# Strassen's scheme for four more blocks of the first up projection and two more of the second, in a hybrid decoder layer

## The chip, the cores and the metric

The kernel runs on one core of a Trainium2 chip. The metric is the time of one execution on the device, in microseconds (us). The core has five engines with a queue each: PE (TensorE, the matmuls, with its weight loads shown apart as PEld), DVE (VectorE), ACT (ScalarE), POOL (GpSimd) and SP (SyncE, which here issues most of the DMAs).

## The reference

One decoder layer on 512 tokens of width 1024, all in float32. A vector c gives nine modulation rows (adaLN): a shift, a scale and a gate for each of three sublayers.

```python
mod = (cs @ w_ada[l] + b_ada[l]).reshape(bsz, N_MOD, D_MODEL)      # cs = silu(c)
h = modulate(x, sh1, sc1)
x = layer_norm(ALPHA * x + 0.5 * g1[:, None, :] * swiglu(h, ffn1_w1[l], ffn1_w3[l], ffn1_w2[l]), ...)
h = modulate(x, sh2, sc2)
m = hybrid_mixer(h, w_in[l], ...)         # SSD heads and S5 heads, one input and one output projection
x = layer_norm(ALPHA * x + g2[:, None, :] * m, ...)
h = modulate(x, sh3, sc3)
x = layer_norm(ALPHA * x + 0.5 * g3[:, None, :] * swiglu(h, ffn2_w1[l], ffn2_w3[l], ffn2_w2[l]), ...)

def swiglu(u, w1, w3, w2):
    return (jax.nn.silu(u @ w1) * (u @ w3)) @ w2                    # 1024 -> 2816 -> 1024
```

## The kernel before, in words

**Products.** A float32 product is made of three matmuls: each operand is split into a high part (a cast on ACT, in `split`, L96) and the rest (a subtraction on DVE, `tt`, L81), and `mm3` (L100) issues hi·hi (L103), hi·lo (L104) and lo·hi (L105) into one PSUM bank. Weights come in by DMA (`raw`), are split into `whi` and `wlo`, and go to PE as the stationary operand or the moving one.

**Stages, in order.** The first modulation and an early start of the up projection (to about 55 us); the first up projection, `up` (to 269.70); the first down projection, `down` (to 395.85), with the layer norm and the transposed, split tokens `hT` of the next sublayer (`to_h`); the mixer, which begins with the z projection from the weight tiles `zw`; the second up projection (its Strassen stage from 672.25 to 835.56); the second down projection.

**Up.** The 2816 hidden columns are 22 blocks of 128. For a block, `up` (L397) runs 8 steps along k, three matmuls of 512 columns each, for w1 and for w3 (48 in all), and `glue` multiplies silu of the one by the other into a half of a tile `g`. After each block it runs `per` steps from a list of jobs, generators that issue small pieces of other work. In the first up projection that job is the S5 setup (`s5_setup`, 71 steps, 4 a block); from block 11 on, `late` puts 3 steps a block of the list `ada` in its place. `ada` holds the loading of the residual and the other modulation rows: two pairs (shift and scale, `ada_pair`) and two gates (`ada_gate`), 70 steps. Each row is summed by `ada_acc` (L267): 8 loads of 512 KB into two tiles `ra`, each followed by a DVE instruction into `acc`. A gate is then split (`gs`), spread over the partitions by four matmuls with `onesr` (L318, L319) and added to its bias in the tile `gate`.

**Strassen.** `up_fast` (L477) does two blocks at a time, w1 or w3 (a unit): 7 products of quarter size in place of 8, each 4 steps along k by three matmuls of 256 columns, 84 in all. DVE makes the sums of weights (`wsum`, `raw`), and combines the products in the tile `cp`. The sums of tokens are made once (`h_sums`, tiles `hs`). Before, this is done for blocks 6 to 21 of the second up projection, 16 units.

**Down.** `down` (L629) makes two halves of 512 output columns, with four token tiles in four banks each, and runs `per` job steps per block (1 before). In the last 6 blocks of the second half the matmuls are held back and go token tile by token tile, so that each tile can be drained (`make_drain`: the gate product `dr`, the sum `res`, statistics `st` and `mv`, the normalisation) while PE works on the next.

**Order.** Each engine takes its own queue in order. The order in the queues is set by a scheduler of tiles from the program's order, priorities and when tiles come free; loads can be moved far ahead.

## Time and profile before

| | |
|---|---|
| median of 3 runs | 965.3 us (965.27 to 965.67) |
| profiled execution | 965.66 us |
| its span | 963.9 us |
| PE busy | 940.7 us (98%) |
| DVE busy | 759.0 us (79%) |
| ACT busy | 449.1 us (47%) |
| POOL busy | 34.0 us (4%) |
| granted clock of TensorE, mean | 0.995 |

The span runs from the first to the last instruction that the profiler records. An engine's busy time is the part of it in which the engine has an instruction under way; a matmul's row is longer than the distance to the next one's start, since matmuls are pipelined. In the rows below a number in square brackets is how long the engine stood idle ahead of an instruction, with what released it. The granted clock is a share of full speed (2.4 GHz). The page gives shares over the whole span, and single places are read from the timeline.

### The profile page before, as it was taken

Reading aid. Unit: us, or ns where it says so; the run is one execution under the profiler, and the core shown is the slowest. Engines: PE = TensorE matmul, PEld = TensorE weight load, DVE = VectorE, ACT = ScalarE, POOL = GpSimd, SP = SyncE. Lnnn points to the kernel's source line nnn. Section 1 sums busy time; section 2 is a strip of 40 time slices with the busy share of each in tenths; the row PEclk is TensorE's granted clock in tenths of the full one; section 3 lists DMA queues with packets and bytes.
Section 4 is the critical chain, followed back from the end, with each engine's and each line's share of the span. In section 5 each row is a group of like instructions: output and inputs, shape, how many; then the busy total and the mean of one; then the engine's idle time right before and its main releaser. Section 6 shows DMA issues by size and latency. Waiting matters only on the chain.

```text
span 963.9 us, 14718 instructions
## 1 busy us (share of the span) xinstructions
PE 940.7 (98%) x5409; PEld 797.0 (83%) x5409; DVE 759.0 (79%) x1522; ACT 449.1 (47%) x882; POOL 34.0 (4%) x73
## 2 busy tenths in 40 slices
PE   8999999999999999999999999999999999999996
PEld 5778888887777878778877777988999999988885
DVE  6579999963686897858995889885788888796946
ACT  3343452635453335545637945432455554634420
POOL 0000000000000000100000110100000000000003
PEclk9999999999999999999999999999999999999998
DMA  9967585453765765362432034521233232543302
GB/s 343 378 182 267 191 278 168 159 175 126 260 199 189 258 220 160 104 218 88 143 121 66 1 100 141 192 92 66 88 108 112 91 130 88 176 152 109 109 1 87
DMA packets 75577, 147.92 MB, mean 153 GB/s; under 512 B 11632, under 2 KB 28656, under 8 KB 74992
## 3 DMA queue, kind: packets, MB, share of 16 engines
q1 hardware_dynamic: 75216, 146.94, 46.1%
q8 instruction: 42, 0.69, 0.3%
q14 instruction: 31, 0.25, 0.1%
q10 hardware_dynamic: 288, 0.04, 0.0%
HBM read 137.52 MB, written 9.44 MB: 152 GB/s over the span
## 4 chain that ended last, share of the span: by engine, by line
PE 84%; DVE 6%; ACT 3%; issue 2%; DMA 2%; POOL 1%; SPq 0%; DVEq 0%; POOLq 0%; ACTq 0%
PE ps L103 27%; PE ps L104 27%; PE ps L105 27%; DMA ew<-in_up_dram 1%; DVE cv L90 1%; PE ps L980 1%; DVE wlo L81 1%; ACT whi L96 1%; DMA b_ada<-in_badaT_dram 1%; DVE s5X L81 0%; POOL rsx L170 0%; DMA raw<-in_w_in_dram 0%; PE ps L253 0%; PE ps L295 0%; DVE s5t L81 0%
## 5 line engine op out<-in xcount | busy, mean ns | idle before, releaser
L96 ACT CAST whi<-raw 128x1024 fp32r<-128x1024 f32 (+1 forms) x155 | 155.0, 1007 | 212.0 <-PE ps L104 98.4
L81 DVE TENSOR_TENSOR wlo<-raw,whi 128x1024 fp32r<-128x1024 f32 (+1 forms) x155 | 179.3, 1168 | 44.6 <-ACT whi L96 44.1
L103 PE MATMUL ps<-hT,whi 128*128 128x512 f32 x448 | 177.0, 396 | 2.4 <-ACT hT L1498 2.4
L104 PE MATMUL ps<-hT,whi 128*128 128x512 f32 x448 | 174.7, 390 | 0.1
L105 PE MATMUL ps<-hT,wlo 128*128 128x512 f32 x448 | 174.5, 390 | 0.0
L103 PE MATMUL ps<-whi,ghl 128*128 128x512 f32 x320 | 125.2, 391 | 0.0
L104 PE MATMUL ps<-wlo,ghl 128*128 128x512 f32 x320 | 124.5, 389 | 0.0
L105 PE MATMUL ps<-whi,ghl 128*128 128x512 f32 x320 | 124.3, 389 | 0.0
L103 PEld LDWEIGHTS ps<-hT,whi 128*128 128x128 f32 x448 | 83.9, 188 | 23.9 <-issue 3.2
L105 PEld LDWEIGHTS ps<-hT,wlo 128*128 128x128 f32 x448 | 84.1, 188 | 17.8
L104 PEld LDWEIGHTS ps<-hT,whi 128*128 128x128 f32 x448 | 84.2, 188 | 17.1 <-DVE hT L81 0.5
L103 PE MATMUL ps<-hx,whi 128*128 128x256 f32 (+1 forms) x320 | 97.5, 305 | 0.7 <-DVE cp L90 0.6
L104 PE MATMUL ps<-hx,whi 128*128 128x256 f32 (+1 forms) x320 | 97.4, 304 | 0.0
L105 PE MATMUL ps<-hx,wlo 128*128 128x256 f32 (+1 forms) x320 | 97.3, 304 | 0.0
L90 DVE SCALAR_TENSOR_TENSOR acc<-ra,cs,acc 128x1024 f32<-128x1024 f32 (+2 forms) x62 | 71.0, 1145 | 19.3 <-DMA ra<-in_w_ada_dram 18.6
L96 ACT CAST ghl<-g 128x512 fp32r<-128x512 f32 x88 | 53.2, 619 | 50.1 <-PE ps L105 38.8
L103 PEld LDWEIGHTS ps<-whi,ghl 128*128 128x128 f32 x320 | 60.1, 188 | 14.8 <-issue 2.5
L105 PEld LDWEIGHTS ps<-whi,ghl 128*128 128x128 f32 x320 | 60.1, 188 | 12.7
L104 PEld LDWEIGHTS ps<-wlo,ghl 128*128 128x128 f32 x320 | 60.1, 188 | 12.1
L81 DVE TENSOR_TENSOR ghl<-g,ghl 128x512 fp32r<-128x512 f32 x88 | 58.2, 687 | 12.7 <-ACT ghl L96 12.7
L103 PEld LDWEIGHTS ps<-hx,whi 128*128 128x128 f32 x320 | 61.1, 191 | 3.9 <-issue 0.8
L105 PEld LDWEIGHTS ps<-hx,wlo 128*128 128x128 f32 x320 | 61.2, 191 | 2.5
(471 smaller groups left out, 1690.9 us busy)
## 6 DMA issues: line engine op xcount, KB each, us to landing
ra<-in_w_ada_dram SPq DMA_DIRECT2D x56, 512.0 KB, 4.5
raw<-in_up_dram SPq DMA_DIRECT2D x49, 512.0 KB, 4.3
raw<-in_ffn_w_dram SPq DMA_DIRECT2D x44, 512.0 KB, 4.2
raw<-in_up_dram SPq DMA_DIRECT2D x64, 256.0 KB, 3.8
ra<-in_ada_dram SPq DMA_DIRECT2D x16, 512.0 KB, 7.8
...
```

The costliest lines, as they stand in the source:

```text
L81: self.nc.vector.tensor_tensor(out=out, in0=a, in1=b, op=op)
L90: self.nc.vector.scalar_tensor_tensor(out=out, in0=a, scalar=s, in1=b, op0=op0, op1=op1, **k)
L96: keep(self.nc.scalar.copy(out=hi, in_=src))
L103: mm(o, lh, rh, start=first, stop=False, **k)
L104: mm(o, lh, rl, start=False, stop=False, **k)
L105: self.last_mm = mm(o, ll, rh, start=False, stop=last, **k)
L980: nc.tensor.matmul(pv[32 * r:32 * r + 32, j, :], M[:, n, r, 32 * j:32 * j + 32], rhs[:, r, :], start=(n == 0), stop=(n == 2))
```

## The change

Blocks 18 to 21 of the first up projection are done by `up_fast` (`FAST1 = 18`), 4 units; in the second up projection the Strassen stage begins at block 4 rather than 6 (`FAST = 4`), 18 units. The S5 setup goes at 6 steps a block, its scratch is released before the sums of tokens take their space, and the `ada` list starts at block 13 (`late=(ada, 3, 13)`). Beside blocks 16 and 17 run the sums of tokens and the first loads and sums of weights (`lead`). During the 4 units one `ada` step follows each unit, and `down` takes 7 `ada` steps in 5 blocks. `cp` moves from the pool of temporaries to pools of its own, `g` tiles can come from a list of spares, and `identr` is cast on ACT in the mixer rather than on DVE at the start. The branches with `add` are not taken; the sums and splits of weights of a unit stay as they were, and their functions are left out below.

```diff
--- before.py
+++ after.py
@@ -381,10 +382,13 @@
             yield
+    def g_tile(self, gp):
+        return self.spare.pop(0) if self.spare else gp.tile([P, 2, S], F32, tag="g", bufs=NF // 2, name=self.nm("g"))
     def glue(self, gp, g, f, pa, pb):
...
         if f % 2 == 0:
-            self.gt = gp.tile([P, 2, S], F32, tag="g", bufs=NF // 2, name=self.nm("g"))
+            self.gt = self.g_tile(gp)
         s = self.tmp.tile([P, 512], F32, tag="t2", name=self.nm("sl"))
@@ -540,9 +550,9 @@
                 self.tt(gt[:, 0, 256:512], gt[:, 0, 256:512], bank[:, 0:256], MUL)
-        load(0)
-        yield
-        load(1)
+        load(0, 0), load(0, 1)
+        yield
+        load(1, 0), load(1, 1)
         yield
@@ -552,14 +562,16 @@
             if j == 0:
-                gt = gts.pop() if gts else gp.tile([P, 2, S], F32, tag="g", bufs=NF // 2, name=self.nm("g"))
+                gt = self.g_tile(gp)
                 g.extend((gt[:, 0, :], gt[:, 1, :]))
-            cp = self.tmp.tile([P, 4, 256], F32, tag="t4", name=self.nm("cp"))
+            cp = sp.tile([P, 3, 256], F32, tag="cp", bufs=2, name=self.nm("cp"))
             p1, u2, p5 = [cp[:, n] for n in range(3)]
...
             prep_c(u)
+            if add:
+                load(u + 2, 0)
             C = self.bank()
@@ -567,14 +579,14 @@
                 prep_a(u + 1)
-            else:
+            elif not add:
                 last()
-            prep_d(u)
-            if u + 2 < len(units):
-                load(u + 2)
+            if not add:
+                prep_d(u)
+                load(u + 2, 0), load(u + 2, 1)
             prod(u, A, "t2", new[1], False)
             nc.scalar.copy(out=u2, in_=A[:, 0:256])
-            self.step(jobs, 1)
+            self.step(jobs, per)
             B = self.bank()
@@ -643,7 +662,8 @@
                                  f == 0, f == nk - 1)
-                    self.step(jobs, per)
+                    slot += 1
+                    self.step(jobs, slot * per // 5 - (slot - 1) * per // 5)
             for t in range(NT):
@@ -1085,6 +1105,8 @@
         nc.scalar.copy(out=self.mask4, in_=bc(self.mask, (1, 4)))
+        self.identr = dp.tile([P, P], F32R, name="identr")
+        nc.scalar.copy(out=self.identr, in_=self.ident)
         for g in range(2):
@@ -1099,8 +1121,6 @@
                                 pattern=[[-1, P]], channel_multiplier=1)
-        self.identr = self.cp.tile([P, P], F32R, name="identr")
-        nc.vector.tensor_copy(self.identr, self.ident)
         self.hsel = self.cp.tile([NC * NH, NH], F32, name="hsel")
@@ -1446,10 +1466,11 @@
         L.early = len(L.wq)
-        L.want_up(ins['up1'], EARLY)
         TAIL = 4
         HALVES = 2
-        FAST = 6
+        FAST1 = 18
+        FAST = 4
+        L.want_up(ins['up1'], EARLY, nf=FAST1)
         def g_alloc():
@@ -1462,10 +1483,14 @@
         g1, g2, g3, m2, m3 = [], [], [], [], []
-        L.want_down(NF, ins['ffn1_w2'][0])
-        L.wlimit = len(L.wq)
-        L.want_mixer()
-        L.want_up(ins['up2'], (), HALVES, g_alloc, FAST)
+        wsum = [L.gates.tile([P, 1024], F32, tag="gate", bufs=2, name="wsum1")]
+        def down1():
+            L.want_down(NF, ins['ffn1_w2'][0])
+            L.wlimit = len(L.wq)
+            L.want_mixer()
+            L.want_up(ins['up2'], (), HALVES, g_alloc, FAST)
+            L.wahead(L.wi + 2)
         hctx, gctx, pctx, fctx, xctx = [ExitStack() for _ in range(5)]
@@ -1538,11 +1563,26 @@
             L.glue(gp, g, f, pss[f, 0], pss[f, 1])
+        L.spare = [L.g_tile(gp) for _ in range(NF // 2 - (len(g) + 1) // 2)]
         jobs = [L.s5_setup(pre)]
         ada = [xres(), L.ada_gate(2, 0.5, g1), L.ada_pair(3, m2), L.ada_pair(6, m3), L.ada_gate(5, 1.0, g2)]
-        L.up(hT, gp, g, f0, jobs, 4, late=(ada, 3, 11), done=pss[f0, 0])
+        L.up(hT, gp, g, f0, jobs, 6, late=(ada, 3, 13), done=pss[f0, 0], nf=FAST1 - 2)
         L.step(jobs, 1000)
         pctx.close()
+        sctx = ExitStack()
+        sp = sctx.enter_context(tile_pool("f1"))
+        hs = [sp.tile([P, 2, 4, 2, P], F32R, tag="hs", bufs=3, name=f"hs1{k}") for k in range(3)]
+        quarter = lambda k, t: hT[:, 2 * t:2 * t + 2, 4 * k:4 * k + 4]
+        z = L.tmp.tile([P, 1024], F32, tag="t4", name="hsum").rearrange("p (a q) -> p a q", a=2)
+        jobs = [L.h_sums(quarter, hs, L.spare[-2:] + [z])]
+        fast = L.up_fast(quarter, hs, wsum[0], sp, gp, g, ins['up1'], FAST1, down1, ada, 1)
+        lead = [(next(fast) for _ in range(4))]
+        L.up(hT, gp, g, FAST1 - 2, jobs, 4, late=(lead, 4, FAST1 - 1), nf=FAST1)
+        L.step(jobs, 1000)
+        L.step(lead, 4)
+        next(fast)
+        ada.insert(0, fast)
+        sctx.close()
         def ln_cols(lg, lb, m):
@@ -1575,7 +1615,7 @@
             L.to_h(hT2, t, res[t], *GB)
-        L.down(NF, getl_of(g, gl), L.make_drain(res, lambda: g1[0], ln1), 6, ada, 1)
+        L.down(NF, getl_of(g, gl), L.make_drain(res, lambda: g1[0], ln1), 6, ada, 7)
         L.step(ada, 1000)
@@ -1602,11 +1642,17 @@
             L.wahead(L.wi + 2)
-        gts = []
-        jobs = [L.h_sums(hx, hs, fp, gts), L.ada_gate(8, 0.5, g3)]
-        fast = L.up_fast(hx, hs, fp, gts, g, ins['up2'], FAST, down2, jobs)
+        wsum2 = L.gates.tile([P, 1024], F32, tag="gate", bufs=2, name="wsum2")
+        quarter = lambda k, t: hx[k][:, 2 * t:2 * t + 2]
+        def sums():
+            own = [L.g_tile(fp) for _ in range(3)]
+            yield from L.h_sums(quarter, hs, own)
+            L.spare = own
+        jobs = [sums(), L.ada_gate(8, 0.5, g3)]
+        fast = L.up_fast(quarter, hs, wsum2, sp, fp, g, ins['up2'], FAST, down2, jobs, 1)
         lead = [(next(fast) for _ in range(4))]
-        L.up(hT3[0], fp, g, 0, jobs, 4, halves=HALVES, late=(lead, 4, FAST - 1), nf=FAST)
+        L.up(hT3[0], fp, g, 0, jobs, 5, halves=HALVES, late=(lead, 4, FAST - 1), nf=FAST)
         L.step(lead, 4)
```

Line numbers of the change are up to 1 higher than before in the places quoted here. Three places show how the queues move.

DVE at the end of the first down projection, before: the last split of `g` (`ghl`), the four splits of the z weights, and the first drain (`dr`).

```order
L81 TENSOR_TENSOR ghl_3849<-g_2880,ghl_3849 128x512
L81 TENSOR_TENSOR zw_4024<-raw_3784,zw_4024 128x1024
L81 TENSOR_TENSOR zw_4027<-raw_3828,zw_4027 128x1024
L81 TENSOR_TENSOR zw_4030<-raw_3836,zw_4030 128x1024
L81 TENSOR_TENSOR zw_4035<-raw_3844,zw_4035 128x1024
L81 TENSOR_TENSOR dr_3870<-ps_3481,gate_1847 128x512
L81 TENSOR_TENSOR wdtr<-wdt,wdtr 128x8x8
```

DVE after the last drain, in the change: the tokens' last `hT` for the first tiles, the normalisation of the last token tile (`res_122`), the split of the attention gate's sum (`gs`, from `acc_3970`), its two additions into `gate_3968`, and the first splits of the z weights.

```order
L82 TENSOR_TENSOR hT_3172<-tf_4225,hT_3172 128x4x128
L88 TENSOR_SCALAR res_122<-res_122,mv_4252,rs_4254 128x1024
L88 TENSOR_SCALAR tf_4225<-ps_4237,G_4168,B_4169 128x128
L86 TENSOR_SCALAR gate_6628<-gate_6628 128x1024
L82 TENSOR_TENSOR hT_3172<-tf_4225,hT_3172 128x4x128
L82 TENSOR_TENSOR gs_4263<-acc_3970,gs_4262 128x1024
L91 SCALAR_TENSOR_TENSOR gate_3968<-ps_4266,gate_3968 128x512
L91 SCALAR_TENSOR_TENSOR gate_3968<-ps_4270,gate_3968 128x512
L82 TENSOR_TENSOR zw_4279<-raw_4023,zw_4279 128x1024
L82 TENSOR_TENSOR zw_4282<-raw_4068,zw_4282 128x1024
```

The z splits stand behind all four drains and behind the end of the attention gate; before, they stood ahead of the first drain.

PE at the same place, before: the last down matmul, eight transposes, the first z matmuls.

```order
L105 MATMUL ps_3484<-whi_3824,ghl_3849 128x512
L339 MATMUL ps_3986<-ident,res_121 128x128 x4
L339 MATMUL ps_3997<-ident,res_121 128x128 x4
L103 MATMUL ps_4059<-zw_4024,hT_2995 128x512
L104 MATMUL ps_4059<-zw_4024,hT_2995 128x512
```

The same in the change.

```order
L106 MATMUL ps_3705<-whi_4064,ghl_4089 128x512
L340 MATMUL ps_4226<-ident,res_120 128x128 x4
L340 MATMUL ps_4237<-ident,res_120 128x128 x4
L319 MATMUL ps_4266<-gs_4262,onesr 128x512
L319 MATMUL ps_4270<-gs_4262,onesr 128x512
L320 MATMUL ps_4266<-gs_4263,onesr 128x512
L320 MATMUL ps_4270<-gs_4263,onesr 128x512
L104 MATMUL ps_4314<-zw_4279,hT_3172 128x512
L105 MATMUL ps_4314<-zw_4279,hT_3172 128x512
```

Four matmuls of the gate (`gs` by `onesr`) stand between the transposes and the first z matmul.

DVE in the first unit of the new Strassen stage, in the change (`acc` is the modulation row, `cp` combines the products, `ps_2688` is the bank that the unit's last product needs, `wlo`, `wsum` and `raw` are weights).

```order
L91 SCALAR_TENSOR_TENSOR acc_3259<-ra_3305,cs,acc_3259 128x1024
L82 TENSOR_TENSOR wlo_2729<-raw_2620,whi_2728 128x512
L91 SCALAR_TENSOR_TENSOR acc_3259<-ra_3308,cs,acc_3259 128x1024
L82 TENSOR_TENSOR cp_2687<-cp_2687,ps_2754 128x256
L91 SCALAR_TENSOR_TENSOR cp_2687<-cp_2687,ps_2707 128x256
L91 SCALAR_TENSOR_TENSOR acc_3259<-ra_3326,cs,acc_3259 128x1024
L82 TENSOR_TENSOR wlo_2783<-raw_2641,whi_2782 128x1024
L91 SCALAR_TENSOR_TENSOR cp_2687<-cp_2687,ps_2688 128x256
L82 TENSOR_TENSOR wlo_2816<-wsum_113,whi_2815 128x1024
L82 TENSOR_TENSOR raw_2641<-raw_2641,wsum_113 128x512
```

Three accumulations of `acc_3259`, each with a load of its own, stand among the unit's splits and combinations.

## Rows read from the trace of the kernel before

**Rows 1.** Page: busy us (share of the span) and instructions of each engine.
```profile
PE 940.7 (98%) x5409; PEld 797.0 (83%) x5409; DVE 759.0 (79%) x1522; ACT 449.1 (47%) x882; POOL 34.0 (4%) x73
```

**Rows 2.** Stretches: busy us (count) of PE, PEld, DVE, ACT, POOL; clock, DMA, GB/s.
```profile
90.00:100.00 10.00, 10.00 (x46) 8.29 (x45) 10.00 (x54) 3.78 (x12) 0.00 (x0) 1.00 0.79 274
...
700.00:750.00 50.00, 50.00 (x419) 50.00 (x418) 42.14 (x62) 27.05 (x44) 0.00 (x0) 1.00 0.32 106
270.00:396.00 126.00, 126.00 (x562) 101.54 (x561) 102.24 (x132) 56.84 (x82) 1.59 (x4) 1.00 0.63 198
```

**Rows 3.** Timeline of PE, first up projection: start, us, instruction.
```profile
59.83 0.39 PE L105 MATMUL ps<-hT,wlo 128*128 128x512 f32 x1
...
72.30 0.39 PE L103 MATMUL ps<-hT,whi 128*128 128x512 f32 x1
```

**Rows 4.** Timeline of PE, Strassen stage of the second up projection.
```profile
699.73 0.28 PE L103 MATMUL ps<-hx,whi 128*128 128x256 f32 x1
...
711.25 0.28 PE L103 MATMUL ps<-hs,whi 128*128 128x256 f32 x1
```

**Rows 5.** Timeline of PE, end of that stage (in brackets: idle before, releaser).
```profile
833.52 0.28 PE L105 MATMUL ps<-hs,wlo 128*128 128x256 f32 x1
834.41 0.36 PE L103 MATMUL ps<-hx,whi 128*128 128x256 f32 x1 [0.61 <-DVE cp L90]
...
835.56 0.40 PE L103 MATMUL ps<-whi,ghl 128*128 128x512 f32 x1
...
837.64 0.39 PE L103 MATMUL ps<-whi,ghl 128*128 128x512 f32 x1
```

**Rows 6.** Timeline of PE, end of the first up projection.
```profile
269.47 0.39 PE L105 MATMUL ps<-hT,wlo 128*128 128x512 f32 x1
269.70 0.39 PE L103 MATMUL ps<-whi,ghl 128*128 128x512 f32 x1
```

**Rows 7.** Waits of DVE (us, times, longest us); instructions on tile `ra`, 276 to 300.
```profile
DVE acc L90 <- DMA ra<-in_w_ada_dram: 18.6, 18, 3.4
...
L90 DVE SCALAR_TENSOR_TENSOR acc<-ra,cs,acc x7: 1280/1285/1286, 277.1 to 295.2; 128x1024 f32<-128x1024 f32 x7
...
DMA to landing us min/median/max: 3.6/4.4/5.0
```

**Rows 8.** Groups of DVE, 45 to 290: busy us, mean ns, idle before, releasers.
```profile
L81 DVE TENSOR_TENSOR wlo<-raw,whi 128x1024 fp32r<-128x1024 f32 x43 | 52.3, 1221 | 12.1 <-ACT whi L96 11.9
```

**Rows 9.** Timeline of DVE, end of the first down projection.
```profile
378.65 4.63 DVE L81 TENSOR_TENSOR zw<-raw,zw 128x1024 fp32r<-128x1024 f32 x4 [1.11 <-ACT zw L96]
...
395.93 0.68 DVE L672 BATCH_NORM_STATS2 st<-res 128x6 f32<-128x512 f32 x1
396.53 0.39 DVE L87 TENSOR_SCALAR tf<-ps,G,B 128x128 f32<-128x128 f32 x1
396.84 0.20 DVE L675 BATCH_NORM_AGGREGATE mv<-st 128x2 f32<-128x12 f32 x1
...
398.04 0.81 DVE L87 TENSOR_SCALAR res<-res,mv,rs 128x1024 f32<-128x1024 f32 x1 [0.72 <-POOL rs L171]
...
399.36 0.69 DVE L81 TENSOR_TENSOR dr<-ps,gate 128x512 f32<-128x512 f32 x1
```

**Rows 10.** Timeline of PE, from the first down projection to z.
```profile
395.85 1.03 PE L339 MATMUL ps<-ident,res 128*128 128x128 f32 x8
397.63 0.50 PE L103 MATMUL ps<-zw,hT 128*128 128x512 f32 x1 [0.74 <-ACT hT L96]
...
399.50 0.50 PE L105 MATMUL ps<-zw,hT 128*128 128x512 f32 x1 [1.14 <-DVE hT L81]
```

**Rows 11.** PE after a gap in the mixer (timeline), and stretches with their clock.
```profile
493.85 0.65 PE L980 MATMUL ps<-s5X,s5M 128*32 128x128 f32 x8 [2.08 <-DVE s5X L81]
...
397.00:400.00 3.00, 1.23 (x4) 0.75 (x5) 2.28 (x6) 3.00 (x7) 0.79 (x2) 1.00 0.00 0
494.00:497.00 3.00, 3.00 (x60) 3.00 (x59) 3.00 (x5) 1.30 (x2) 0.00 (x0) 0.50 0.42 153
```

More of the change, by code (lines that the diff above doesn't have):

```diff
@@ L436, in up, with h_sums @@
                 pss.append(ps)
-    def h_sums(self, hq, new, gp, gts):
+    def h_sums(self, v, new, gts):
         nc = self.nc
-        v = lambda k, t: hq[k][:, 2 * t:2 * t + 2]
         hi, lo = lambda a: a[:, :, :, 0, :], lambda a: a[:, :, :, 1, :]
-        for _ in range(3):
-            gts.append(gp.tile([P, 2, S], F32, tag="g", bufs=NF // 2, name=self.nm("g")))
         x, y, z = [t.rearrange("p a (b q) -> p (a b) q", q=P).rearrange("p (t k) q -> p t k q", t=2)
@@ L475, in h_sums, with up_fast, load @@
         self.s4 = lambda: split(y, v(0, 1))
-    def up_fast(self, hq, new, gp, gts, g, w, f0, last, jobs):
+    def up_fast(self, v, new, c, sp, gp, g, w, f0, last, jobs, per, add=False):
         nc = self.nc
         units = [(f, j) for f in range(f0, NF, 2) for j in range(2)]
-        v = lambda k, t: hq[k][:, 2 * t:2 * t + 2]
         raws, ops, hold = {}, {}, {}
-        def load(u):
+        def load(u, kh):
+            if u >= len(units):
+                return
             f, j = units[u]
-            ts = []
-            for kh in range(2):
-                t = self.raw.tile([P, 1024], F32, tag="raw", name=self.nm("raw"))
-                for m in range(2):
-                    nc.sync.dma_start(out=t[:, 512 * m:512 * m + 512].rearrange("p (k n) -> p k n", k=4),
-                                      in_=w[f + m][:, j, 4 * kh:4 * kh + 4])
-                ts.append(t)
-            raws[u] = ts
+            t = self.raw.tile([P, 1024], F32, tag="raw", name=self.nm("raw"))
+            for m in range(2):
+                x = t[:, 512 * m:512 * m + 512].rearrange("p (k n) -> p k n", k=4)
+                nc.sync.dma_start(out=x, in_=w[f + m][:, j, 4 * kh:4 * kh + 4])
+            if add and kh == 0:
+                nc.gpsimd.dma_start(out=x, in_=w[f][:, j, 0:4], accum_op=ADD)
+            raws.setdefault(u, []).append(t)
         def split(u, raw, names):
@@ L506, in up_fast @@
         lo_, hi_ = slice(0, 512), slice(512, 1024)
-        c = self.gates.tile([P, 1024], F32, tag="gate", bufs=2, name="wsum")
         def prep_a(u):
             a, b = raws[u]
-            self.tt(c[:, lo_], a[:, hi_], b[:, hi_], ADD)
-            self.tt(a[:, hi_], a[:, hi_], a[:, lo_], ADD)
+            if not add:
+                self.tt(c[:, lo_], a[:, hi_], b[:, hi_], ADD)
+                self.tt(a[:, hi_], a[:, hi_], a[:, lo_], ADD)
             split(u, a, ("b11", "t1"))
-            self.tt(c[:, hi_], a[:, hi_], b[:, hi_], ADD)
+            if not add:
+                self.tt(c[:, hi_], a[:, hi_], b[:, hi_], ADD)
         def prep_b(u):
-            split(u, raws[u][1], ("b21", "b22"))
+            a, b = raws[u]
+            if add:
+                self.tt(c[:, hi_], a[:, hi_], b[:, hi_], ADD)
+                self.tt(c[:, lo_], c[:, hi_], a[:, lo_], SUB)
+            split(u, b, ("b21", "b22"))
+            if add:
+                nc.gpsimd.dma_start(out=b[:, lo_], in_=c[:, hi_], accum_op=ADD)
         def prep_c(u):
             split(u, c, ("t3", "t2"))
-            b = raws[u][1]
-            self.tt(b[:, lo_], b[:, lo_], c[:, hi_], ADD)
+            if not add:
+                b = raws[u][1]
+                self.tt(b[:, lo_], b[:, lo_], c[:, hi_], ADD)
         def prep_d(u):
@@ L562, in up_fast @@
             prep_c(u)
+            if add:
+                load(u + 2, 0)
             C = self.bank()
@@ L569, in up_fast @@
                 prep_a(u + 1)
[L570 removed]
+            elif not add:
                 last()
[L572 to L574 removed]
+            if not add:
+                prep_d(u)
+                load(u + 2, 0), load(u + 2, 1)
             prod(u, A, "t2", new[1], False)
             nc.scalar.copy(out=u2, in_=A[:, 0:256])
[L577 removed]
+            self.step(jobs, per)
             B = self.bank()
@@ L584, in up_fast @@
                 self.tt(gt[:, 0, 0:256], gt[:, 0, 0:256], p1, MUL)
+            if add:
+                prep_d(u)
+                load(u + 2, 1)
             prod(u, C, "b22", v(0, 1), False)
@@ L588, in up_fast @@
                 prep_b(u + 1)
+            elif add:
+                last()
             prod(u, A, "t3", new[2], False)
@@ L627, in want_down, with down @@
                           (lambda sl=sl: gate()[:, sl]) if gate and hf == 1 else None)
-    def down(self, nk, getl, drain, tail, jobs=None, per=1):
+    def down(self, nk, getl, drain, tail, jobs=None, per=5):
+        slot = 0
         for hf in range(2):
```

1 line of the change is left out of this document (added).

## The prediction

> **What bounds the kernel now.** I began with the busy shares of the page. PE (TensorE) is busy for 940.7 of 963.9 us and VectorE (DVE) for 759.0 [rows 1]. So the time is PE's work plus the 23 us in which PE stands still, and a change is worth what it takes off PE's queue less what it makes PE wait. The stretches say which engine would be next. In the first up projection (90 to 100) PE and DVE are both full; in the Strassen stage (700 to 750) DVE runs 42.14 of 50 us; in the first down projection (270 to 396) PE is never idle and DVE has 102.24 of 126 [rows 2]. PE's waits are therefore looked for where a stage ends, and DVE's where a load is late.
>
> The profiled execution took 965.66 us, 1.76 outside its span, and 0.36 above the median of 965.3. The sum is made against 965.66, and 0.36 comes off at the end. Of this kernel no more than 0.2%, 1.9 us, can be told from no change.
>
> **Matmuls removed: -4.8 us.** One unit (two blocks, one of w1 and w3) costs 48 x 512 columns directly and 84 x 256 columns by Strassen. In a full stretch the 512-column matmuls start at 59.83 and, 55 later, at 72.30: 0.2267 us each [rows 3]. The 256-column ones start at 699.73 and, 96 later, at 711.25: 0.120 each [rows 4]. A unit goes from 48 x 0.2267 = 10.88 to 84 x 0.120 = 10.08 and saves 0.80; four new units in the first up projection and two in the second save 4.8.
>
> The Trainium skill ("TensorE: Matmul & The Clock Gate", section "Wait — 56ns, not 53.3ns?") gives start-to-start as the columns over 2.4 GHz and about 2.5 ns more, which is 215.7 ns for 512 and, worked out the same way, an estimate of 109.2 for 256. By it a unit would save 48 x 0.2157 - 84 x 0.1092 = 1.18 us and the six 7.1. The trace has both slower, and the 256-column ones by more; the trace decides.
>
> **Closing a second Strassen stage: +0.9 us (0.5 to 1.5).** The last product of the last unit waits for the subtraction that frees its bank: the matmul expected at 833.64 starts at 834.41, 0.77 lost. From there to 835.56 the rows show starts at 0.12 with 0.07 on top, and from 835.56 to 837.64 nine 512-column matmuls, 2.04 us worth in 2.08 [rows 5]. The kernel before goes from up to down in block form without such a gap: 269.47, then 269.70 [rows 6]. So the price is new.
>
> **Inside that stage: +1.3 us (0 to 4).** DVE's sums and splits for Strassen are joined by accumulations for adaLN (`acc<-ra`), which wait on their loads with everything behind them waiting too. In the second up projection few such loads fall among the units. Here, by the order shown above, `acc_3259<-ra_3326` stands right ahead of the subtraction into `cp_2687` that frees the bank for the next unit's closing product. PE reaches that product 2.88 us (24 x 0.120) after the subtraction's input is done. The accumulations waited 18.6 us in all for their loads, the worst 3.4 [rows 7]. A wait of 3.4 and two instructions of 1.2 in the way exceed 2.88 by about 3, once; usually it fits. I take 1.3, between none and the 4 us of two bad waits, nearer to none, since 18.6 us over 18 waits is one each.
>
> **S5 setup at 6 steps a block: 0 (0 to 3).** The same instructions run, earlier; the adaLN work starts 2 blocks later and gives its place up (8 accumulations less, some 10 us, between blocks 3 and 13). What hides it: PE in the first up projection shows no wait, and DVE's weight splits in that stage themselves wait for casts (11.9 us `<-ACT whi`) [rows 8], so they run ahead of PE. If that cover goes, PE pays DVE's excess directly. The larger step of 5 jobs in the second up projection and the moved cast of `identr` go with it, at 0: the sums there run beside 512-column matmuls with DVE under its limit.
>
> **From the down projection to the mixer: +6.7, and +3 (0 to 7) on top.** Before, `ada` is done well inside the down projection. Before DVE's first drain stand the four splits of the z weights: 378.65, 4.63 us [rows 9]; so when the last down matmul ends (E = 395.85) PE needs just the normalised tokens. It starts z at 397.63, waits once more, and has the third z matmul at 399.50 [rows 10]; counted back two matmuls of 0.23, z runs as if it had started at 399.04, E + 3.2.
>
> After, 70 adaLN steps are to be done: 9 beside blocks, 4 in the Strassen units, and 38 x 7/5 = 53 in the down projection. That is 66. The last four, the end of the attention gate, come behind the down projection: PE's queue has the four gate matmuls between the last down matmul and z, and DVE's queue has all four drains and this gate ahead of the z splits. From E on DVE must do, in order, with durations from [rows 9] less 0.085, by which rows that follow each other overlap (395.93, 0.68 long, and the next at 396.53): drain 0.60, add 0.60, `tf` 0.32, statistics 0.60 and 0.13, `hT` 0.60, the scaling 0.73 after a wait for POOL of up to 1.00 (0.72 there), `tf` 0.32, gate scale 0.60, `hT` 0.60, the gate split 1.14, a start of PE and its result 0.5, two additions 1.20, and the z split 1.14: 10.1 us. Only z's second matmul needs that split, so z starts at E + 9.9, and 9.9 - 3.2 = **+6.7**. That holds if DVE is not behind at E. The last two accumulations stand between the drains, and each waits for a load. 17 more of them lie between the first half's drains and the second half's first. Before, seven in a row came from 277.1 to 295.2, 3.0 us apart, with loads of 4.4 us into two buffers [rows 7]: 51 us for the 17. The half lasts 126.15/2 = 63.1 and its first drain comes 12.7 before its end (three tiles of 18 matmuls and the transposes): 50.4. So they come out about even, and any longer wait pushes the drains. I add 3, less than one load of 4.4, between 0 and one and a half loads.
>
> **The clock: +1.5 (0 to 2).** After 2.08 us of standing still PE's granted clock was 0.50 (1.2 GHz of 2.4) from 494 to 497, 3 us in which half was lost, 1.5. After the shorter gaps at 397 to 400 it stayed at 1.00 [rows 11]. The new gap is longer than either, so I take the first.
>
> **Sum:** -4.8 + 0.9 + 1.3 + 0 + 6.7 + 3 + 1.5 = +8.6; 965.66 + 8.6 - 0.36 = **973.9 us**. With the low ends (0.5, 0, 0, 6.7 less 1 for pieces that may overlap, 0, 0) it is 966.7; with the high ends (1.5, 4, 0, 6.7, 7, 2) it is 981.7. Likeliest case's own range: 967 to 982.
>
> **Rival 1, faster: a 256-column matmul costs half of a 512-column one.** Place: the six units. If 0.120 is not the engine's pace but that of the Strassen stage's operands, and new units run at 0.2267/2 = 0.1133, a unit takes 9.52 and saves 1.36; six save 8.2. With the low ends of closing (0.5) and transition (5.7) this gives 965.3 - 8.2 + 6.2 = 963.3. It decides below a pace of about 0.116. The page named above has the halves at 109.2, which speaks for it; against it stand 96 steps on end at an even 0.120 [rows 4]. Chance 0.10.
>
> **Rival 2, no difference.** DVE is up to date at E, the clock does not fall, the Strassen stage closes at 0.5 and has no wait inside: 965.3 - 4.8 + 0.5 + 5.7 = 966.7. For it: two accumulations less before the drains than I fear, and 4.63 us of z splits no longer ahead of them. Chance 0.10.
>
> **Rival 3, much slower: DVE saturates in the first up projection.** At 90 to 100 it already runs 10.00 of 10 [rows 2], and six steps of S5 a block add half as much again. If the weight splits fall behind, PE waits in up to 13 blocks; at 1 us a block that is 973.9 + 13 = 986.9. Against it: [rows 8], and fewer accumulations. It decides if the splits' waits for ACT vanish. Chance 0.08. That the change skips work is not a rival: its queue holds 6 x 84 matmuls for 6 x 48.
>
> **Chances.** Likeliest 0.72, rival 1 0.10, rival 2 0.10, rival 3 0.08. Below 963.4: rival 1's better half and a little from better ends, 0.11. Within 963.4 to 967.2: 0.10. Slower: 0.79. The range goes from 963.0, just past rival 1, to 982; rival 3 is left out.
>
> **What would show it.** The units of the first up projection take 10.08 us each; between PE's last down matmul and its first z matmul lie gate matmuls and 8 to 15 us; DVE's z splits start after all drains; granted clock 0.50 follows. A gap under 5 us there, or PE waits before block 13, would prove the sum wrong.

## The result and the profile after

The changed kernel takes 987.8 us (median of three, 987.5 to 990.0) against 965.3: ratio 1.0233, 95% interval 1.0219 to 1.0246. The forecast was 973.9 with a range to 982; the side was right, the size was not. The profiled execution's span is 985.8 us, 21.9 longer than before.

The page of the kernel after, busy time by engine and the granted clock in 40 slices (tenths of full speed):

```profile
PE 943.8 (96%) x5625; PEld 807.2 (82%) x5625; DVE 801.3 (81%) x1590; ACT 471.3 (48%) x920; POOL 34.3 (3%) x73
...
PEclk9999899999999999889999999999999999999998
```

PE is busy 3.1 us longer than [rows 1], although it has fewer columns to do, and stands still for 42 us, where it was 23. The clock dips in the fifth slice (98 to 123 us) and about 410; only the second place was foreseen. Cut at PE's own rows, the stages are (us, profiled executions):

| stage, from PE's row to PE's row | before | after | difference |
|---|---|---|---|
| start to the first down matmul (`whi,ghl`) | 269.70 | 273.88 | +4.18 |
| first down projection | 126.15 | 133.73 | +7.58 |
| its end to the end of z's first token tile | 8.78 | 20.65 | +11.87 |
| rest of the mixer, to the first matmul of the second up projection | 198.51 | 198.35 | -0.16 |
| second up projection | 232.42 | 230.96 | -1.46 |
| rest | 128.34 | 128.23 | -0.11 |

Three stages lose. **The S5 setup.** PE's timeline in the first up projection, the first line of the kernel before, the others of the kernel after, and below them stretches of the kernel after with their clock:

```profile
115.83 1.03 PE L870 MATMUL ps<-ident,bd 128*128 128x128 f32 x8
...
96.90 0.39 PE L106 MATMUL ps<-hT,wlo 128*128 128x512 f32 x1
99.74 0.64 PE L890 MATMUL ps<-ident,bd 128*128 128x128 f32 x4 [2.45 <-ACT bd L877]
101.21 1.08 PE L890 MATMUL ps<-ident,bd 128*128 128x128 f32 x4 [0.83 <-ACT bd L877]
101.94 0.78 PE L104 MATMUL ps<-hT,whi 128*128 128x512 f32 x1
102.52 0.63 PE L105 MATMUL ps<-hT,whi 128*128 128x512 f32 x1
102.94 0.63 PE L106 MATMUL ps<-hT,wlo 128*128 128x512 f32 x1
...
100.00:104.00 4.00, 3.17 (x13) 2.56 (x12) 4.00 (x36) 2.23 (x5) 0.00 (x0) 0.53 0.30 111
104.00:108.00 4.00, 4.00 (x12) 3.14 (x12) 4.00 (x20) 1.95 (x11) 1.05 (x2) 0.62 0.36 109
108.00:112.00 4.00, 4.00 (x20) 3.28 (x19) 1.60 (x7) 2.40 (x6) 0.00 (x0) 1.00 0.60 203
```

PE has the eight matmuls of `ident` by `bd` 16 us earlier than before (99.74; before, 115.83, without a wait), and waits 3.3 us for them. Then the clock is 0.50, so that matmuls start 0.42 apart (102.52, 102.94) rather than 0.227, to about 107. `bd` is a copy that ACT makes of `p0r` to `p3i`, which DVE makes. DVE's timeline there:

```profile
91.95 1.28 DVE L91 SCALAR_TENSOR_TENSOR acc<-ra,cs,acc 128x1024 f32<-128x1024 f32 x1
93.15 0.17 DVE L82 TENSOR_TENSOR s5t<-s5co 128x16 f32<-128x16 f32 x1
93.24 0.22 DVE L82 TENSOR_TENSOR s5u<-a1r,p0i 128x64 f32<-128x64 f32 x1
...
93.98 1.28 DVE L91 SCALAR_TENSOR_TENSOR acc<-ra,cs,acc 128x1024 f32<-128x1024 f32 x1
95.18 0.17 DVE L82 TENSOR_TENSOR s5t<-e1r 128x16 f32<-128x16 f32 x1
...
99.68 0.22 DVE L82 TENSOR_TENSOR p3i<-s5u,s5u 128x64 f32<-128x64 f32 x1
```

DVE has no idle moment, and between its small S5 instructions stand accumulations of the first adaLN gate, which the scheduler moves up here, long before block 13. Six of them stand ahead of the first products (79.21 to 93.98). Before the change six stood at nearly the same times (79.75 to 94.49), so it is the products that moved towards them. The second wait, of 0.83, is in part ACT's: `p3i` is done at 99.90, and its copy starts at 100.57, behind a cast of weights.

**The down projection.** PE's timeline of the kernel after, a stretch with its clock, and DVE's timeline ahead of the second of these waits:

```profile
321.37 1.05 PE L296 MATMUL ps<-acc,ones 128*32 128x512 f32 x4 [1.62 <-DVE acc L91]
...
375.80 1.08 PE L296 MATMUL ps<-acc,ones 128*32 128x512 f32 x4 [2.45 <-DVE acc L91]
376.81 0.80 PE L104 MATMUL ps<-whi,ghl 128*128 128x512 f32 x1
...
378.00:379.00 1.00, 1.00 (x4) 0.81 (x3) 0.75 (x1) 0.02 (x1) 0.00 (x0) 0.50 0.86 348
...
372.45 1.28 DVE L91 SCALAR_TENSOR_TENSOR acc<-ra,cs,acc 128x1024 f32<-128x1024 f32 x1 [1.39 <-DMA ra<-in_w_ada_dram]
373.65 0.69 DVE L82 TENSOR_TENSOR ghl<-g,ghl 128x512 fp32r<-128x512 f32 x1
374.46 1.29 DVE L91 SCALAR_TENSOR_TENSOR acc<-ra,cs,acc 128x1024 f32<-128x1024 f32 x1
```

PE's queue reaches the matmuls of a modulation row (`acc,ones`) before DVE has its last accumulation; the one ahead of that waited 1.39 us for its load. After the second wait the clock is 0.50 as well.

**From down to z.** PE's timeline, the first line of the kernel before, the others of the kernel after, and DVE's of the kernel after:

```profile
397.96 0.40 PE L104 MATMUL ps<-zw,hT 128*128 128x512 f32 x1
...
407.61 1.03 PE L340 MATMUL ps<-ident,res 128*128 128x128 f32 x8
414.20 1.22 PE L319 MATMUL ps<-gs,onesr 128*128 128x512 f32 x2 [5.55 <-ACT gs L97]
418.25 1.22 PE L320 MATMUL ps<-gs,onesr 128*128 128x512 f32 x2 [2.83 <-DVE gs L82]
419.27 0.63 PE L104 MATMUL ps<-zw,hT 128*128 128x512 f32 x1
421.56 0.80 PE L105 MATMUL ps<-zw,hT 128*128 128x512 f32 x1 [1.66 <-DVE zw L82]
...
392.36 1.28 DVE L91 SCALAR_TENSOR_TENSOR acc<-ra,cs,acc 128x1024 f32<-128x1024 f32 x1 [1.91 <-DMA ra<-in_w_ada_dram]
399.87 1.28 DVE L91 SCALAR_TENSOR_TENSOR acc<-ra,cs,acc 128x1024 f32<-128x1024 f32 x1 [1.22 <-DMA ra<-in_w_ada_dram]
410.47 0.68 DVE L82 TENSOR_TENSOR dr<-ps,gate 128x512 f32<-128x512 f32 x1
416.97 1.22 DVE L82 TENSOR_TENSOR gs<-acc,gs 128x1024 fp32r<-128x1024 f32 x1
420.29 4.62 DVE L82 TENSOR_TENSOR zw<-raw,zw 128x1024 fp32r<-128x1024 f32 x4
...
423.00:424.00 1.00, 1.00 (x4) 0.80 (x3) 1.00 (x2) 0.00 (x0) 0.00 (x0) 0.50 0.71 182
```

These answer to [rows 9] and [rows 10]: the down projection ends at 407.61, DVE drains the last tile from 410.47, and z's second matmul starts at 421.56, 13.95 us after the down projection, where it was 2.1 before (397.96).

The new Strassen stage behaves as its model did [rows 5]: one wait inside and one at its end.

```profile
244.04 0.39 PE L104 MATMUL ps<-hT,whi 128*128 128x256 f32 x1 [1.10 <-DVE cp L91]
272.37 0.36 PE L104 MATMUL ps<-hT,whi 128*128 128x256 f32 x1 [0.60 <-DVE cp L91]
272.81 0.28 PE L104 MATMUL ps<-hT,whi 128*128 128x256 f32 x1
...
273.76 0.28 PE L106 MATMUL ps<-hT,wlo 128*128 128x256 f32 x1
273.88 0.40 PE L104 MATMUL ps<-whi,ghl 128*128 128x512 f32 x1
```

From its first row (231.26) to the first down matmul it takes 42.6 us, for 4 x 10.08 = 40.3. The pace is 0.119 to 0.120 (272.81 to 273.76, 8 steps).

### The profile page after: what moved, and what is told of

It reads as the page before. It is cut to its first block, busy times and chain, and to the rows that moved or that the text cites. A ratio compares the mean times of both kernels' runs of the same rounds, so it can differ in the third digit from the quotient of the medians.

```text
span 985.8 us, 15291 instructions
## 1 busy us (share of the span) xinstructions
PE 943.8 (96%) x5625; PEld 807.2 (82%) x5625; DVE 801.3 (81%) x1590; ACT 471.3 (48%) x920; POOL 34.3 (3%) x73
## 4 chain that ended last, share of the span: by engine, by line
PE 56%; DVE 12%; DMA 5%; issue 4%; ACT 4%; POOL 1%; DVEq 0%; POOLq 0%; ACTq 0%
PE ps L104 18%; PE ps L105 18%; PE ps L106 18%; DMA ra<-in_w_ada_dram 4%; DVE acc L91 2%; DVE wlo L82 2%; DVE cv L91 1%; ACT whi L97 1%; DVE s5X L82 1%; DVE ghl L82 1%; DVE res L91 1%; DVE s5v L982 1%; DVE s5t L82 1%; POOL rsx L171 0%; DVE st L692 0%
## 5 line engine op out<-in xcount | busy, mean ns | idle before, releaser
L97 ACT CAST whi<-raw 128x1024 fp32r<-128x1024 f32 (+1 forms) x161 | 158.5, 992 | 188.9 <-PE ps L105 66.9
L82 DVE TENSOR_TENSOR wlo<-raw,whi 128x1024 fp32r<-128x1024 f32 (+1 forms) x161 | 183.2, 1150 | 46.2 <-ACT whi L97 45.7
L104 PE MATMUL ps<-hT,whi 128*128 128x512 f32 (+1 forms) x448 | 171.2, 384 | 3.5 <-ACT hT L1523 1.7
L105 PE MATMUL ps<-hT,whi 128*128 128x512 f32 (+1 forms) x448 | 169.5, 378 | 0.1
L106 PE MATMUL ps<-hT,wlo 128*128 128x512 f32 (+1 forms) x448 | 169.4, 378 | 0.0
L104 PEld LDWEIGHTS ps<-hT,whi 128*128 128x128 f32 x448 | 84.9, 190 | 22.2 <-issue 3.8
L105 PEld LDWEIGHTS ps<-hT,whi 128*128 128x128 f32 x448 | 85.3, 190 | 15.0 <-DVE hT L82 0.5
L104 PE MATMUL ps<-hx,whi 128*128 128x256 f32 (+1 forms) x320 | 94.0, 294 | 0.6 <-DVE cp L91 0.6
L105 PE MATMUL ps<-hx,whi 128*128 128x256 f32 (+1 forms) x320 | 94.0, 294 | 0.0
L106 PE MATMUL ps<-hx,wlo 128*128 128x256 f32 (+1 forms) x320 | 93.9, 294 | 0.0
L97 ACT CAST ghl<-g 128x512 fp32r<-128x512 f32 x88 | 53.2, 619 | 50.8 <-PE ps L106 42.6
L104 PE MATMUL ps<-hs,whi 128*128 128x256 f32 x264 | 74.7, 283 | 0.0
L105 PE MATMUL ps<-hs,whi 128*128 128x256 f32 x264 | 74.7, 283 | 0.0
L106 PE MATMUL ps<-hs,wlo 128*128 128x256 f32 x264 | 74.7, 283 | 0.0
L105 PEld LDWEIGHTS ps<-wlo,ghl 128*128 128x128 f32 x320 | 60.5, 189 | 12.4
```

What stands on the lines that cost most here:

```text
L82: self.nc.vector.tensor_tensor(out=out, in0=a, in1=b, op=op)
L97: keep(self.nc.scalar.copy(out=hi, in_=src))
L104: mm(o, lh, rh, start=first, stop=False, **k)
L105: mm(o, lh, rl, start=False, stop=False, **k)
L106: self.last_mm = mm(o, ll, rh, start=False, stop=last, **k)
```

## The experiments

Ratios are to the kernel before on the same chip, whose runs lay between 965.0 and 967.8 us, with medians of 966.7 to 967.2 (965.3 beside the changed kernel); so times of different experiments are compared to no better than 2 us, and single places by their rows.

### S5 at six steps, alone

```diff
-        L.up(hT, gp, g, f0, jobs, 4, late=(ada, 3, 11), done=pss[f0, 0])
+        L.up(hT, gp, g, f0, jobs, 6, late=(ada, 3, 11), done=pss[f0, 0])
```

> The kernel before with one number changed: the S5 setup at 6 steps a block, no new Strassen units, the adaLN list from block 11 as before. Theory A (six steps put the first products of the S5 setup, the matmuls of ident by bd, on PE before VectorE has made them; PE stands still 3.3 us and then runs some 6.6 us at half clock): 965.3 + 6.5 = about 972, with a wait of 2 to 3 us at the first ident,bd matmul near 100 us and a granted clock of 0.50 behind it. Rival B (that wait comes from the later start of the adaLN list or from the other moved work): 965 to 966, no such wait.

Measured: 972.0 us, ratio 1.0057 (1.0040 to 1.0074). Its PE timeline:

```profile
99.48 0.63 PE L870 MATMUL ps<-ident,bd 128*128 128x128 f32 x4 [2.82 <-ACT bd L857]
...
158.31 0.66 PE L870 MATMUL ps<-ident,bd 128*128 128x128 f32 x4 [1.11 <-ACT bd L857]
160.13 0.66 PE L870 MATMUL ps<-ident,bd 128*128 128x128 f32 x4 [1.17 <-ACT bd L857]
```

In the profiled execution, which took 973.0 us, the up projection is 7.9 us longer (277.62 for 269.70), the rest of the kernel as before. Theory A holds: the denser setup costs this by itself. Part of it sits at a second place, near 160 us, which was not expected. There the accumulations of the list from block 11 stand on DVE as well (128.99 to 161.98). The changed kernel, whose list begins at block 13, has its products of 159.04 without a wait.

### The accumulations left out

The sums of the later modulation rows keep their first part only.

```diff
         for k in range(KD):
+            if 0 < k:
+                if k == KD - 1:
+                    box.append(acc)
+                yield
+                continue
             w = self.accp.tile([P, D], F32, tag="ra", bufs=2, name=self.nm("ra"))
```

> The changed kernel with the adaLN sums of the chunks 2 to 8 cut to the first of eight loads (seven loads and seven accumulations of each are left out; splits, matmuls and steps stay). Theory A (the accumulations and their loads are what VectorE lacks, at the S5 setup and in the down projection; behind the down projection the order itself costs 6.7 us and the clock some 2): the S5 wait, the two waits for acc in the down projection and the lag of VectorE at its end go, the chain from the drains to z stays: about 972, z's first matmul 9 to 10 us after the last down matmul. Rival B (the S5 setup fills VectorE by itself): the wait near 100 us stays, about 979. Rival C (without late accumulations the end of the down projection is covered as well): about 964.

Measured: 971.5 us, ratio 1.0050 (1.0035 to 1.0065). Theory A. The first down matmul comes at 265.85, 3.85 us earlier than before the change; the down projection takes 127.4; and the end of the down projection to the end of z's first tile takes 18.4, still 9.6 more than before. So neither the S5 instructions nor the order alone make PE wait in the first two places, and the third loss is the order's, with or without late loads.

### The first gate's accumulations left out

The same edit with `if chunk == 2 and 0 < k`.

> The changed kernel with the first adaLN gate's sum cut to the first of eight loads (seven loads and accumulations left out, all of them early in the first up projection). Theory A (the eight accumulations among the first S5 products are what makes them late): the wait at the first ident,bd matmul and the half clock behind it go, all the rest stays: 987.8 - 6.6 = about 981. Rival B (the S5 instructions alone fill VectorE): the wait stays, 985 or more.

Measured: 980.9 us, ratio 1.0157 (1.0139 to 1.0175). Its PE timeline and stretches at the place of the wait:

```profile
96.38 0.39 PE L106 MATMUL ps<-hT,wlo 128*128 128x512 f32 x1
96.61 1.03 PE L895 MATMUL ps<-ident,bd 128*128 128x128 f32 x8
97.40 0.48 PE L104 MATMUL ps<-hT,whi 128*128 128x512 f32 x1
...
266.87 0.40 PE L104 MATMUL ps<-whi,ghl 128*128 128x512 f32 x1
...
100.00:104.00 4.00, 4.00 (x19) 3.34 (x18) 4.00 (x24) 1.64 (x10) 1.05 (x2) 1.00 0.63 236
```

No wait, clock 1.00, and the first down matmul at 266.87 for 273.88: 7.0 us. This shows Theory A: the seven accumulations left out, with their loads, are the difference, and five of them stood ahead of the first products. DVE is full in either kernel (4.00 of 4.00); what counts is what stands in its queue ahead of the product that PE waits for. The down projection is 131.3 here, 2.4 less than in the changed kernel: its two waits for `acc` are 1.45 and 1.81, and the clock stays at 1.00 behind both. So the size of that loss depends also on whether the clock falls.

### S5 at five steps, and at four and then seven

```diff
-        L.up(hT, gp, g, f0, jobs, 4, late=(ada, 3, 11), done=pss[f0, 0])
+        L.up(hT, gp, g, f0, jobs, 5, late=(ada, 3, 11), done=pss[f0, 0])
```

> The kernel before with the S5 setup at 5 steps a block. Theory A (what PE waits for at 6 steps is the amount of VectorE work up to the first ident,bd matmuls, where the first adaLN sum of eight accumulations stands as well; at 5 steps PE comes a block, some 5 us and more, later): a wait under 1 us at the first ident,bd matmul near 105 us, 965 to 968. Rival B (any more than 4 steps makes PE wait about as long): 970 or more.

Measured: 970.4 us, ratio 1.0037 (1.0024 to 1.0051). Theory A missed. The first products come without a wait at 105.35, but the second set makes PE wait:

```profile
158.21 0.38 PE L908 MATMUL ps<-ident,k 128*128 128x128 f32 x1 [2.77 <-ACT k L905]
```

The other form, in the changed kernel, spreads the steps unevenly (`self.step(jobs, part(per(f) if callable(per) else per))`):

```diff
-        L.up(hT, gp, g, f0, jobs, 6, late=(ada, 3, 13), done=pss[f0, 0], nf=FAST1 - 2)
+        L.up(hT, gp, g, f0, jobs, lambda f: 4 if f < 9 else 7, late=(ada, 3, 13), done=pss[f0, 0], nf=FAST1 - 2)
```

> The changed kernel with the S5 setup at 4 steps in blocks 3 to 8 and 7 in blocks 9 to 15; the rest as it is. Theory A (only the first ident,bd matmuls come too early for VectorE, which has the first adaLN sum of eight accumulations to do as well): they come some two blocks later, the wait near 100 us and the 0.50 behind it go, 987.8 - 6.6 = about 981. Rival B (VectorE has no time left for 71 steps in 13 blocks whatever their spread): the waits move to blocks 9 to 15, 985 to 990.

Measured: 985.1 us, ratio 1.0188 (1.0174 to 1.0201): 2.7 less than the changed kernel's 987.8, in place of 6.6, and in the up projection alone 1.5 (first down matmul at 272.39 for 273.88). The wait near 100 is gone (`ident,bd` at 116.06), and waits of 2.16 and 2.00 for `ident,k` stand at 157.51 and 183.09. That is nearer to rival B. The first products alone are not the whole of it; any spread tried that ends the setup earlier than at four steps a block makes PE wait somewhere.

### The adaLN list earlier

```diff
-        L.up(hT, gp, g, f0, jobs, 6, late=(ada, 3, 13), done=pss[f0, 0], nf=FAST1 - 2)
+        L.up(hT, gp, g, f0, jobs, 6, late=(ada, 3, 11), done=pss[f0, 0], nf=FAST1 - 2)
```

> The changed kernel with the adaLN list from block 11 rather than 13, so that 72 steps of 70 are done by the end of the down projection and the attention gate's matmuls stand ahead of its last tiles. Theory A (the four steps left over cost the 11 to 12 us between down and z): that gap falls to the 3 to 4 us of before, the waits for acc inside the down projection stay or grow by a few us: 977 to 981. Rival B (VectorE is late there whatever stands in the queue): gap of 8 us or more, 986 to 989.

Measured: 980.0 us, ratio 1.0139 (1.0115 to 1.0164). Theory A. The gate's matmuls stand inside the down projection (394.74), z starts at 414.55, 0.8 us after the end of the down projection, and its first tile is done 6.9 us after it, 13.8 sooner than in the changed kernel. The up projection loses 4.8 more (first down matmul at 278.69, a wait of 2.94 at 160.36). The down projection stays long, 135.1, with four waits of 0.87 to 1.88 for `acc` and `gs`.

### More steps in the down projection

```diff
-        L.down(NF, getl_of(g, gl), L.make_drain(res, lambda: g1[0], ln1), 6, ada, 7)
+        L.down(NF, getl_of(g, gl), L.make_drain(res, lambda: g1[0], ln1), 6, ada, 9)
```

> The changed kernel with 9 adaLN steps in 5 blocks of the down projection rather than 7. Theory A (PE waits in the down projection because the list asks for an accumulation every 1.94 us, at 9 in 5 every 1.51 us, where loads and VectorE give one in 2.6 to 3.0): the gap to z goes (minus 8 to 9 us), but the waits of PE for acc and gs inside the down projection grow from 4 us to 8 to 15 us: 978 to 988. Rival B (those waits are chance, not pace): they stay at about 4 us, 977 to 979.

Measured: 986.6 us, ratio 1.0206 (1.0185 to 1.0227). Theory A's mechanism: the waits of PE for `acc` and `gs` inside the stage are 1.52, 7.95, 1.18 and 1.48, 12.1 in all, for 4.1 (1.62 and 2.45), and the stage takes 143.5 us. PE's timeline at the largest, and DVE's ahead of it:

```profile
344.56 1.92 PE L296 MATMUL ps<-acc,ones 128*32 128x512 f32 x4 [7.95 <-DVE acc L91]
...
340.85 2.47 DVE L692 BATCH_NORM_STATS2 st<-res 128x6 f32<-128x512 f32 x4
343.23 1.27 DVE L91 SCALAR_TENSOR_TENSOR acc<-ra,cs,acc 128x1024 f32<-128x1024 f32 x1
```

Here the last accumulation stands behind the drains of the first half in DVE's queue, and PE waits for both. The gain at the end was smaller than expected: from there to z's first tile 12.4 us, with a wait of 2.87 for `hT` and the low clock again.

### One step a block in the down projection

```diff
-        L.up(hT, gp, g, f0, jobs, 6, late=(ada, 3, 13), done=pss[f0, 0], nf=FAST1 - 2)
+        L.up(hT, gp, g, f0, jobs, 6, late=(ada, 6, 11), done=pss[f0, 0], nf=FAST1 - 2)
...
-        L.down(NF, getl_of(g, gl), L.make_drain(res, lambda: g1[0], ln1), 6, ada, 7)
+        L.down(NF, getl_of(g, gl), L.make_drain(res, lambda: g1[0], ln1), 6, ada, 5)
```

> The changed kernel with the adaLN list from block 11 at 6 steps a block, and then one step a block in the down projection (every 2.72 us) as before. Theory A (PE waits in the down projection because accumulations are asked for faster than one in 2.6 to 3.0 us): the down projection takes 126 to 128 us again, for 133.7, and the gap to z is as before; in blocks 11 to 15 the accumulations meet the S5 setup, which costs some 5 to 15 us there. Rival B (the Strassen stage ahead of it is what makes the down projection longer): it stays at 132 or more.

Measured: 969.6 us, ratio 1.0036 (1.0023 to 1.0050), 18 us less than the changed kernel. Theory A: the down projection takes 125.7 us, without a wait for `acc` or `gs`, and z's first tile ends 7.5 after it, less than before. The price in the up projection was below the 5 to 15 expected: the first down matmul at 275.72, 1.8 later than in the changed kernel, with waits of 2.62, 0.84, 1.85 and 1.03 for `ident,bd`. What is left against the kernel before lies in the up projection (275.72 for 269.70), where the S5 setup and the list meet.

### Two cures together

The steps at four and then seven, and the list from block 11 at 3 steps.

> The changed kernel with both cures: S5 steps at 4 and then 7, and the adaLN list from block 11. If the losses add up (theory A): 980 of the run with the list from block 11, less its S5 wait and clock of 7 to 10: 970 to 973. Rival B (7 steps and the accumulations of blocks 11 and 12 meet on VectorE): waits between 120 and 180 us, 976 or more.

Measured: 975.5 us, ratio 1.0090 (1.0070 to 1.0110). Between the two: one wait of 4.14 for `ident,k` at 159.38 takes back a part.

### A smaller first Strassen stage

```diff
-        FAST1 = 18
+        FAST1 = 20
...
-        L.up(hT, gp, g, f0, jobs, 6, late=(ada, 3, 13), done=pss[f0, 0], nf=FAST1 - 2)
+        L.up(hT, gp, g, f0, jobs, 5, late=(ada, 4, 11), done=pss[f0, 0], nf=FAST1 - 2)
...
-        L.down(NF, getl_of(g, gl), L.make_drain(res, lambda: g1[0], ln1), 6, ada, 7)
+        L.down(NF, getl_of(g, gl), L.make_drain(res, lambda: g1[0], ln1), 6, ada, 6)
```

> The changed kernel with a smaller Strassen stage in the first up projection: blocks 20 and 21 only, so that the S5 setup has 15 blocks at 5 steps; the adaLN list from block 11 at 4 steps, 6 in 5 blocks in the down projection. Theory A: 965.3 - 1.6 (second up projection) - 1.6 (two units) + 0.6 (closing) = 962.7 where nothing waits, and up to 4 more where the S5 products still come a little early: 963 to 967, with the first ident,bd matmul near 105 us, no gap over 2 us between down and z. Rival B (any denser S5 setup fills VectorE): 969 or more.

In this kernel a scratch tile of the token sums is also the tile of blocks 18 and 19, so values of these blocks and sums differ from the reference; the instructions are the same. Measured: 971.8 us, ratio 1.0049 (1.0035 to 1.0064), above the range: the same second set of S5 products as at five steps costs a wait of 3.69 at 158.80. The time to z's first tile is 8.8 us, as before. The down projection, with 6 steps in 5 blocks, takes 126.3 us, with one wait of 0.34 for `acc`.

### The second up projection alone

```diff
-        FAST = 6
+        FAST = 4
...
-        L.up(hT3[0], fp, g, 0, jobs, 4, halves=HALVES, late=(lead, 4, FAST - 1), nf=FAST)
+        L.up(hT3[0], fp, g, 0, jobs, 5, halves=HALVES, late=(lead, 4, FAST - 1), nf=FAST)
```

> The kernel before with only the second up projection changed: Strassen from block 4, sums of tokens at 5 steps a block. Theory A (two units at 10.08 for 10.88 us, no new wait): 1.6 us less than before, ratio 0.9983. Rival B (a unit costs half of a direct one's pace by columns, 9.52): 2.7 us less, 0.9972. Rival C (the sums, squeezed into four blocks, make PE wait): no gain or a loss.

Measured: 968.2 us, ratio 1.0014 (1.0004 to 1.0024): not the gain, and so not theory A. The second up projection takes 234.1 us, 1.7 more than before, with one new wait and the low clock behind it (PE's timeline, stretch):

```profile
717.59 0.39 PE L103 MATMUL ps<-hx,whi 128*128 128x256 f32 x1 [1.75 <-ACT whi L96]
...
720.00:721.00 1.00, 1.00 (x7) 1.00 (x7) 1.00 (x2) 0.35 (x1) 0.00 (x0) 0.50 0.76 221
```

In the changed kernel this wait is absent. Here `cp` still shares a pool of temporaries with the split of the last gate (`gs`). DVE's rows fit that: the gate's last accumulation is at 633.86, and its split comes 80 us later, between the sums of weights (`raw`, `wsum`) that ACT's cast `whi` needs. In the run that follows, it comes right behind its sum. The first line is of this run, the second of the next:

```profile
713.45 1.22 DVE L81 TENSOR_TENSOR gs<-acc,gs 128x1024 fp32r<-128x1024 f32 x1
...
636.08 1.23 DVE L82 TENSOR_TENSOR gs<-acc,gs 128x1024 fp32r<-128x1024 f32 x1 [0.20 <-ACT gs L97]
```

The last run takes the change's form of the second up projection, with `cp` in its own pool (and `identr` moved, which makes the room), and everything of the first as before:

> The changed kernel without its part in the first up projection: no Strassen units there, the S5 setup at 4 steps, the adaLN list from block 11 and one step a block in the down projection, as before; Strassen from block 4 of the second up projection, with the change's own pool for cp. Theory A (the wait of 1.75 us in the run with that part alone came from cp sharing the temporaries with the last gate; with its own pool two units save 1.6 us): 1.4 to 1.6 us less than the kernel before on the same chip, ratio 0.9983 to 0.9986, faster than both kernels. Rival B (the wait has another cause): it stays, ratio 1.001.

```diff
-            cp = self.tmp.tile([P, 4, 256], F32, tag="t4", name=self.nm("cp"))
+            cp = sp.tile([P, 3, 256], F32, tag="cp", bufs=2, name=self.nm("cp"))
...
-        self.identr = self.cp.tile([P, P], F32R, name="identr")
+        self.identr = dp.tile([P, P], F32R, name="identr")
...
-        FAST = 6
+        FAST = 4
```

Measured: 963.3 us, ratio 0.9968 (0.9955 to 0.9980), the fastest of all: its five runs (963.2 to 963.7) lie below every run of the kernel before (965.0 and more). The second up projection takes 230.9 us for 232.4, 1.5 less, and the wait is gone. The ratio says more than that because the runs of before spread over 2.7 us on this chip; the profiled spans, 962.0 and 963.9, differ by 1.9. That sharing `cp`'s pool made the wait fits both runs and the place of `gs` in them; the two kernels differ in smaller ways too (the tiles of the token sums, the order of the loads' calls), which were not taken apart.

## Why the prediction was wrong

Term by term, measured from the rows above:

| term of the sum | foreseen | measured | from |
|---|---|---|---|
| matmuls removed | -4.8 | about -4.7 | two units 1.46 in the second up projection, pace 0.120 in the first |
| closing and inside of the new Strassen stage | 0.9 + 1.3 | 2.3 | 42.6 for 40.3 |
| S5 at 6 steps a block | 0 (0 to 3) | 7.0 | 273.88 against 266.87 without seven of the first gate's accumulations |
| inside the down projection | not there | about 6.5 | 7.58 less 1.05 of matmuls moved there from the up projection; 4.1 are waits, some 1.7 the clock |
| from down to z, with the clock | 6.7 + 3 + 1.5 | 11.9 | 20.65 against 8.78 |

These add up to 23.0. Two groups of adaLN matmuls left the up projection. Four `acc,ones`, 1.05 in all, are now in the down projection, where the table has taken them off; four `gs,onesr`, 0.93, are now between down and z, inside the 11.9. So 0.9 comes off, and 0.3 more for the stages not listed (-0.16 and -0.11): 21.8, of the 21.9 measured.

**The step that failed first: "S5 setup at 6 steps a block: 0".** Its cover was that DVE's weight splits run ahead of PE [rows 8]. They do, but they were not what would be late: PE takes the S5 products themselves, and its queue has their matmuls a fixed number of blocks after the setup's start, whoever is ready. The text had argued that 8 accumulations leave this stretch; those that stayed stood in front of the first products, where DVE had no idle moment [rows 2], and the denser setup brought PE to these products 16 us earlier. A cover read from a group over 245 us says nothing about the stretch of 10 us in which the queue is full. Rival 3 named this engine and place, and nearly the time, 987, but by waits in every block. Instead there were two waits at one place (2.45 and 0.83), and nearly half of the 7.0 was the low clock behind them. The range has a slip too: its upper end adds the high ends of the other terms but not the 3 of this one, which makes 984.7 of 981.7; 987.8 lies above that as well.

**The second: the down projection was costed only at its end.** Seven steps in 5 blocks are one every 1.94 us (13.6 us for 7). A row of a pair takes ten steps, two of them without an accumulation, so its matmuls are asked for 19.4 us after those of the row before. The prediction itself had accumulations coming 3.0 us apart [rows 7]; after the change the eight of a row came 2.75 apart (300.80 to 320.03), 22 us for eight. It used the number to say when the list would end, and did not ask who waits if it is late: PE, at `acc,ones`, inside its own queue. The runs with 9 steps (a row every 15.1 us: waits of 12.1), with 6 (22.7: one of 0.34) and with 5 (27.2: none) show that it is the pace, with two reservations: the longest wait at 9 steps also had drains of the first half ahead of the accumulation, and the runs with 6 and 5 steps have fewer rows left for this stage.

**What held.** The transition came within 0.7 us of its term: the chain of drains, gate and z splits by its rows, a lag of DVE of about 2.7 us (its last drain at 410.47, where the last down matmul's row ends at 407.77) for the 3 taken, and the low clock. Leaving out the accumulations leaves 9.6 of the 11.9, where the sum had 8.2 without a lag (6.7 and 1.5), and takes off 2.3, where it had 3; so part of the close agreement is two small misses that cancel. Moving the gate ahead of the last tiles takes all of it away. The front matter says that the adaLN list takes the place of the S5 steps; it runs beside them, which makes blocks 13 to 15 denser than the text assumed. The wait inside the new Strassen stage came as its term had it: the accumulation of 241.24 waited 2.08 for its load, ahead of the subtraction into `cp` that PE waits for at 244.04. Rival 1 fell: the new units run at 0.119 to 0.120 a matmul, as in [rows 4]. The Trainium skill ("TensorE: Matmul & The Clock Gate", section "Wait — 56ns, not 53.3ns?") leads to an estimate of 0.109; the trace disagrees in both stages.
